# Feed-forward layers with seven products for eight: the third weight sum moved from VectorE to an accumulating DMA, and a new table of spacings

## Chip, cores and metric

One core of a Trainium2 chip. The time is device microseconds (us) for one execution of the whole kernel, as the median of several runs; lower is better. The engines are named as the profile names them: PE (TensorE, matmuls), ACT (ScalarE), DVE (VectorE), POOL (GpSimd) and SP (the engine that issues most DMAs).

## What is computed

Two decoder layers over 256 tokens of width 2048 in float32: attention with its projections, and behind each attention a feed-forward part. The change is in that last part alone:

```python
D_MODEL = 2048
SEQ = 256
D_FF = -(-(8 * D_MODEL) // (3 * 256)) * 256        # 5632

def swiglu(h, w_gate, w_up, w_down):
    return (jax.nn.silu(h @ w_gate) * (h @ w_up)) @ w_down

# in layer_a and in layer_b alike, behind the attention:
    h = h + o
    return h + swiglu(rms_norm(h, norm_ffn), w_gate, w_up, w_down)
```

The tokens' activations stay on the chip; every weight is read once from memory and used for all 256 tokens.

## The kernel before

**Three matmuls for one product.** To keep float32 accuracy each operand is split into a high and a low part. `split` does it with two instructions: ACT rounds (`hi`), and DVE subtracts (`lo`, line 81). `mm3` then runs hi x hi, lo x hi and hi x lo (lines 89 to 91). PE has 512 columns in each of these matmuls. A split of a 128x1024 weight tile gives `whi` and `wlo`, one of a whole quarter gives `qhi` and `qlo` (128x2048 where four pairs of rows are taken together, 128x1536 where it is three).

**Groups.** The 5632 columns of the hidden layer are eleven blocks of 512, in three portions of four, four and three blocks (`PORTIONS`). A gate/up group computes one block: four PSUM banks (two halves of the tokens, gate and up). After the blocks of a portion, two down groups multiply that portion's hidden values with `w_down` and add to `h`. So the row of groups in a layer is: gate/up 0 to 3, down, down, gate/up 4 to 7, down, down, gate/up 8 to 10, down, down. In layer b the last portion's down projection is made by plain matmuls at the very end (`final`).

**Seven products for eight.** In a group some pairs of 128-row blocks (`npr` pairs: 4 in a gate/up group, `NPH` = 3 in a down group) are not multiplied as four times two blocks but by a scheme of seven products on sums of blocks. The remaining rows are "chunks": each chunk is one 128x1024 weight tile and 12 matmuls (`plain`). A gate/up group has 8 chunks (the first of a layer 16, and no products), a down group has 10 (6 in the last portion). The seven products are the steps `s0` to `s6`. Each needs a weight operand made from the four quarters q11, q12, q22 and q21 in tiles `qa`, `qb` and `qc`, which are loaded by SP (1024 KB for a gate/up group, 768 KB for a down group):

- `s0`: q11 in `qa`
- `s1`: `qa` + q12 (a DVE addition)
- `s2`: `qa` + q22 (a DVE addition); then POOL issues a DMA that adds q21 from memory onto `qa`
- `s3`: q12 + q22 in `qb` (a DVE addition)
- `s4`: q22 in `qc`;  `s5`: `qa` with q21 added;  `s6`: q21, loaded into `qb`

There is one buffer of each of `qa`, `qb` and `qc`, two of `qhi`/`qlo`, three of `whi`/`wlo` and four of the raw chunks. So the q11 of the next group is loaded into `qa` only when DVE has made the `qlo` of `s5`, and a split waits until PE has finished the product, or the chunk three back, whose buffer it takes.

**What sets the order.** `run_groups` runs the chunks of group g interleaved with the seven steps of group g+1: the table in `spacing` says how many chunks stand ahead of `s0`, `s1`, ... `s6`. With 8 chunks it was (2, 1, 1, 2, 0, 2, 0), so the order on PE was two chunks, `s0`, one chunk, `s1`, one chunk, `s2`, two chunks, `s3`, `s4`, two chunks, `s5`, `s6`, and then the next group's first chunks. PE's order is that of the code; the other engines' and SP's order comes from a scheduler at build time, and each engine runs its list strictly in order. `done` finishes a group: for a gate/up group two silu and two multiplications, after which `heads` transposes the new hidden values during the next group (from its sixth tick on; a tick is a third of a chunk's 12 matmuls or one row pair of a product) and, for a pair of rows that takes part in the seven products, forms their sums on DVE (lines 287 to 290, `xf`). For a down group `done` is four additions onto `h` (line 1036, or line 335 in the last portion). `keep`, `rest` and the copies from bank to bank combine the products.

Of the kernel before, what the change touches and what calls it, by code (L numbers as in the profile page):

```python
# [44 lines left out]
def decoder_trunk(ctx: ExitStack, tc: tile.TileContext, a: dict, out: bass.AP):  # L45
# [126 lines left out]
    def at(fs, *ticks):  # L172
        assert len(fs) == len(ticks)
        return list(zip(ticks, fs))
# [678 lines left out]
    class Group:  # L853
# [4 lines left out]

        late = False

        def __init__(self, op, quarters, rest, done, rest_done=None):
            self.op, self.q, self.rest, self.done, self.rest_done = op, quarters, rest, done, rest_done
            self.bank = {}
            self.r = None
            self.plain_only = quarters is None
            if quarters is None:
                for i in range(3):
                    self.new(i)
# [11 lines left out]
        def product(self, b, s, t, side, start=False):  # L880
# [3 lines left out]
            for q in range(npr):  # L884
                mm3(self.bank[b], self.op.slot(q, s), tuple(v[:, q * 512:(q + 1) * 512] for v in hl),
                    start and q == 0, q == npr - 1, True)
                side.tick()

        def keep(self, b):
            t = fq.tile([P, 512], F32, tag="keep", name="keep", bufs=2)  # L890
            with tc.high_priority(offset=URGENT):
                nc.scalar.activation(t, self.bank[b], AF.Copy)
            return t

        def steps(self, side):
            def s0():
                self.qa = self.load(0)
                self.new(1)
                self.product(1, 1, self.qa, side, True)
                with tc.high_priority(offset=URGENT):  # L900
                    nc.scalar.activation(self.new(0), self.bank[1], AF.Copy)

            def s1():
                self.qb = self.load(1)
                nc.vector.tensor_add(self.qa, self.qa, self.qb)
                self.new(2)
                self.product(2, 7, self.qa, side, True)
                self.p5 = self.keep(2)

# [9 lines left out]
            def s3():  # L919
                nc.vector.tensor_add(self.qb, self.qb, self.qc)  # L920
                self.product(1, 4, self.qb, side)
                self.r = fq.tile([P, 512], F32, tag="rest", name="rest")
                with tc.high_priority(offset=URGENT):
                    nc.vector.tensor_sub(self.r, self.p5, self.bank[1])
                if self.rest_done is not None:
                    self.rest_done(self)
# [30 lines left out]

    def spacing(n, late):

        if late:  # L960
            return (4, 1, 0, 1, 0, 2, 0), n - 8
        base = {16: (4, 2, 2, 3, 2, 3, 0), 10: (3, 1, 1, 2, 1, 2, 0), 8: (2, 1, 1, 2, 0, 2, 0), 6: (1, 1, 0, 1, 1, 2, 0)}[n]
        return base, n - sum(base)

    def run_groups(groups):
        for i, g in enumerate(groups):
# [4 lines left out]
            if nxt is not None and nxt.q is not None:  # L971
                base, left = spacing(n, nxt.late)
                for p, s in enumerate(nxt.steps(side)):
                    for _ in range(base[p] + (left if p == 6 else 0)):
                        g.plain(c, side)
                        c += 1
                    if c == n and g.done is not None:
                        side.flush()
                        g.done(g)
                        g.done = None  # L980
                    s()
# [7 lines left out]
    def ffn(pre, op, f_r, last):  # L989
        gq, gs = a[pre + "_gu_q"], a[pre + "_gu_s"]  # L990
        groups = []
        for pi, (b0, b1) in enumerate(PORTIONS):
# [4 lines left out]
            def hop(pi=pi, nk=nk, final=final, hp=hp):  # L997
                if "op" not in hp:
                    x = pair(lambda i: fh.tile([P, HW], F32R, tag=("hThi", "hTlo")[i], name=("hThi", "hTlo")[i]))
                    hp["op"] = Paired(x, NPH, nk, sums=not (final and pre == "b"))  # L1000
                return hp["op"]

            def gate_up(g, j, hop=hop, late=b1 - b0 < 4):
                hb = []
                for tt in range(2):
# [3 lines left out]
                    hb.append(t)  # L1009
                deferred.extend(at(hop().heads(j, hb), *((4, 4) if late and j > 0 else (6, 6))))  # L1010

# [6 lines left out]
            if final and pre == "b":  # L1018
                run_groups(groups)
                last([[a["b_w_down_last"][nb, c] for c in range(nk // CK)] for nb in range(4)], hop().xs, nk)  # L1020
                return
            dq, ds = a[f"{pre}_dn_q"], a[f"{pre}_dn_s{pi}"]
            for n2 in range(2):
# [13 lines left out]

                groups.append(Lazy(n2 == 0 and b1 - b0 < 4, hop, [dq[pi, n2, i] for i in range(4)], [ds[n2, c] for c in range(nk - 2 * NPH)], done, rest_done))
        run_groups(groups)

    class Lazy(Group):
        def __init__(self, late, hop, *args):
            super().__init__(None, *args)
            self.late, self.hop = late, hop

# [228 lines left out]
def _layout(np, i):  # L1274
# [24 lines left out]
    for pre in "ab":  # L1299
# [3 lines left out]
        g[pre + "_gu_q"], g[pre + "_gu_s"] = q[1:], r[1:]  # L1303
        dq = []
        for pi, (b0, b1) in enumerate(PORTIONS):
            w = wd[b0 * 512:b1 * 512].reshape(-1, 2, 2, 512)
            q, r, _ = _pairs(np, w[:, :, 0].reshape(-1, 1024), w[:, :, 1].reshape(-1, 1024), 2, NPH)
            if pre == "b" and pi == len(PORTIONS) - 1:
                g["b_w_down_last"] = _blocks(np, wd[b0 * 512:b1 * 512])
            else:  # L1310
                dq.append(q)
                g[f"{pre}_dn_s{pi}"] = r
        g[pre + "_dn_q"] = np.stack(dq)
    return g
# [26 lines left out]
```

## Time and profile before

| | |
|---|---|
| median of 3 runs | 2041.65 us (2041.49 to 2043.13) |
| the profiled execution | 2039.75 us; its span, first to last instruction, 2038.0 us |
| PE busy | 2006.9 us, 98% of the span |
| DVE busy | 1620.9 us, 80% |
| ACT busy | 1216.3 us, 60% |
| DMA queues | 55.1% (SP's) and 8.3% (POOL's) of the 16 DMA engines' span |

A busy share is an average over stages. "PE busy" counts an engine that has a matmul in flight, and matmuls overlap, so what a wait costs is read from the distance between two matmuls' starts.

### The profile page before, as it was taken

The numbers are of one execution on the slowest core, as the hardware profiler recorded it, in microseconds if no ns is written. First come the engines' busy times: TensorE is split into PE (matmuls) and PEld (weight loads), VectorE is DVE, ScalarE is ACT, GpSimd is POOL, SyncE is SP. The second block draws the span as 40 slices with busy tenths as digits, with TensorE's granted clock in tenths as the row PEclk, the third lists the DMA queues.
The fourth block names the chain that finished last, engine by engine and source line by source line (L and its number), as shares of the span: only waits on it lengthen the run. The fifth ranks groups of instructions, "written<-read, shape, count | busy, mean of one in ns | idle before, by whom it ended". The sixth has DMA issues, their size and how long they took to land.

```text
span 2038.0 us, 25320 instructions
## 1 busy us (share of the span) xinstructions
PE 2006.9 (98%) x9357; PEld 1664.7 (82%) x9357; DVE 1620.9 (80%) x1975; ACT 1216.3 (60%) x1534; POOL 37.2 (2%) x62
## 2 busy tenths in 40 slices
PE   9999999999999999999999999999999999999998
PEld 7898888888888888888887888878888888888886
DVE  6767898778888888888887678788888888888855
ACT  7755566656655566555665555666655566655643
POOL 0000000000000000000000000000000000000000
PEclk9999999999999999999999999999999999999999
DMA  8867633576666676567764754476656776567654
GB/s 309 275 197 232 215 124 116 185 245 213 245 203 218 217 243 238 192 217 225 252 215 136 238 166 156 147 254 217 235 190 211 233 255 224 189 214 242 211 188 150
DMA packets 103100, 429.56 MB, mean 211 GB/s; under 512 B 11968, under 2 KB 12352, under 8 KB 89792
## 3 DMA queue, kind: packets, MB, share of 16 engines
q1 hardware_dynamic: 97632, 395.31, 55.1%
q0 software_dynamic: 5056, 31.59, 8.3%
q8 instruction: 73, 1.20, 0.2%
q10 hardware_dynamic: 288, 1.05, 0.1%
q14 instruction: 51, 0.42, 0.1%
HBM read 423.71 MB, written 4.19 MB: 210 GB/s over the span
## 4 chain that ended last, share of the span: by engine, by line
PE 86%; DVE 8%; issue 2%; ACT 2%; DMA 1%; SPq 0%; POOLq 0%; POOL 0%; ACTq 0%; DVEq 0%
PE mm L91 27%; PE mm L89 27%; PE mm L90 27%; DVE qlo L81 3%; DVE wlo L81 1%; DVE q L920 1%; PE aux L235 1%; ACT qhi L80 1%; DMA q<-in_a_dn_q_dram 1%; PE aux L91 1%; DVE hTlo L81 1%; PE aux L90 1%; PE aux L89 1%; PE aux L316 1%; PE aux L350 0%
## 5 line engine op out<-in xcount | busy, mean ns | idle before, releaser
L80 ACT ACTIVATE whi<-raw 128x1024 fp32r<-128x1024 f32 (+1 forms) x436 | 455.5, 1045 | 408.5 <-PE mm L90 343.6
L81 DVE TENSOR_TENSOR wlo<-raw,whi 128x1024 fp32r<-128x1024 f32 (+1 forms) x436 | 523.7, 1204 | 155.7 <-ACT whi L80 148.7
L81 DVE TENSOR_TENSOR qlo<-q,qhi 128x2048 fp32r<-128x2048 f32 (+1 forms) x210 | 443.1, 2112 | 138.5 <-ACT qhi L80 138.4
L80 ACT ACTIVATE qhi<-q 128x2048 fp32r<-128x2048 f32 (+1 forms) x210 | 372.2, 1775 | 196.3 <-PE mm L90 139.0
L89 PE MATMUL mm<-whi,xhi 128*128 128x512 f32 (+1 forms) x1216 | 474.2, 390 | 3.7 <-ACT xf L304 1.7
L91 PE MATMUL mm<-wlo,xhi 128*128 128x512 f32 (+1 forms) x1216 | 468.4, 385 | 0.0
L90 PE MATMUL mm<-whi,xlo 128*128 128x512 f32 (+1 forms) x1216 | 468.0, 385 | 0.0
L89 PEld LDWEIGHTS mm<-whi,xhi 128*128 128x128 f32 x1216 | 228.7, 188 | 46.2 <-ACT xf L304 2.1
L91 PEld LDWEIGHTS mm<-wlo,xhi 128*128 128x128 f32 x1216 | 228.5, 188 | 46.0
L90 PEld LDWEIGHTS mm<-whi,xlo 128*128 128x128 f32 x1216 | 228.9, 188 | 41.3
L91 PE MATMUL mm<-qlo,xhi 128*128 128x512 f32 x560 | 219.8, 393 | 9.1 <-DVE qlo L81 9.1
L89 PE MATMUL mm<-qhi,xhi 128*128 128x512 f32 x560 | 218.4, 390 | 0.0
L90 PE MATMUL mm<-qhi,xlo 128*128 128x512 f32 x560 | 218.2, 390 | 0.0
L89 PE MATMUL mm<-whi,hThi 128*128 128x512 f32 x464 | 181.5, 391 | 0.0
L91 PE MATMUL mm<-wlo,hThi 128*128 128x512 f32 x464 | 180.9, 390 | 0.0
L90 PE MATMUL mm<-whi,hTlo 128*128 128x512 f32 x464 | 180.8, 390 | 0.0
L84 DVE SCALAR_TENSOR_TENSOR wlo<-raw,gains,whi 128x512 fp32r<-128x512 f32 x160 | 113.8, 748 | 42.9 <-ACT whi L83 42.0
L83 ACT ACTIVATE whi<-raw,gains 128x512 fp32r<-128x512 f32 x160 | 107.6, 716 | 55.9 <-PE mm L90 45.1
L91 PEld LDWEIGHTS mm<-qlo,xhi 128*128 128x128 f32 x560 | 105.2, 188 | 36.4 <-DVE qlo L81 15.0
L90 PEld LDWEIGHTS mm<-qhi,xlo 128*128 128x128 f32 x560 | 105.2, 188 | 22.0
L89 PEld LDWEIGHTS mm<-qhi,xhi 128*128 128x128 f32 x560 | 105.2, 188 | 21.7 <-ACT qhi L80 0.4
L89 PE MATMUL mm<-whi,ohi 128*128 128x512 f32 x256 | 101.6, 397 | 1.6 <-ACT whi L83 1.6
(277 smaller groups left out, 2473.8 us busy)
## 6 DMA issues: line engine op xcount, KB each, us to landing
q<-in_a_gu_q_dram SPq DMA_DIRECT2D x40, 1024.0 KB, 7.0
raw<-in_a_gu_s_dram SPq DMA_DIRECT2D x80, 512.0 KB, 5.0
q<-in_b_gu_q_dram SPq DMA_DIRECT2D x40, 1024.0 KB, 7.0
raw<-in_b_gu_s_dram SPq DMA_DIRECT2D x80, 512.0 KB, 5.2
raw<-in_a_dn_s_dram SPq DMA_DIRECT2D x52, 512.0 KB, 4.6
raw<-in_b_dn_s_dram SPq DMA_DIRECT2D x40, 512.0 KB, 4.8
q<-in_a_dn_q_dram SPq DMA_DIRECT2D x24, 768.0 KB, 5.9
raw<-in_a_w_out_dram SPq DMA_DIRECT2D x32, 512.0 KB, 3.7
```

The lines of the kernel that those rows point to most:

```text
L80: nc.scalar.activation(hi, src, AF.Copy)
L81: nc.vector.tensor_sub(lo, src, hi.bitcast(F32))
L83: nc.scalar.activation(hi, src, AF.Copy, scale=gain)
L84: nc.vector.scalar_tensor_tensor(lo, src, gain, hi.bitcast(F32), op0=ALU.mult, op1=ALU.subtract)
L89: nc.tensor.matmul(o, l[0], r[0], start=start, stop=False, skip_group_check=more)
L90: nc.tensor.matmul(o, l[1], r[0], start=False, stop=False, skip_group_check=more)
L91: nc.tensor.matmul(o, l[0], r[1], start=False, stop=stop, skip_group_check=more)
L235: nc.tensor.transpose(ps[:, i * P:(i + 1) * P], s, ident)
L316: nc.tensor.transpose(ps[:, i * P:(i + 1) * P], tok[tt][:, i * P:(i + 1) * P], ident)
L920: nc.vector.tensor_add(self.qb, self.qb, self.qc)
```

## The change

The sum q12 + q22 is no longer made by DVE: right behind the addition that uses q12, POOL issues a second DMA that adds the third quarter from memory onto `qb`. The table of spacings is new, with no separate one for the last portion. The last portion's down groups take two row pairs into the seven products in place of three (`NPH - final`), so they have 8 chunks, a quarter there has 512 KB, and the weights are laid out accordingly. The load of the first q11 of a layer stands ahead of that layer's first chunks in the code (`fetch`).

```diff
+        def fetch(self):
+            self.qa = self.load(0)
+
...
             def s0():
-                self.qa = self.load(0)
+                if self.qa is None:
+                    self.fetch()
                 self.new(1)
                 self.product(1, 1, self.qa, side, True)
...
                 nc.vector.tensor_add(self.qa, self.qa, self.qb)
                 self.new(2)
                 self.product(2, 7, self.qa, side, True)
+                nc.gpsimd.dma_start(self.qb, self.q[2], accum_op=ALU.add)
                 self.p5 = self.keep(2)
...
             def s3():
-                nc.vector.tensor_add(self.qb, self.qb, self.qc)
                 self.product(1, 4, self.qb, side)
...
-    def spacing(n, late):
-
-        if late:
-            return (4, 1, 0, 1, 0, 2, 0), n - 8
-        base = {16: (4, 2, 2, 3, 2, 3, 0), 10: (3, 1, 1, 2, 1, 2, 0), 8: (2, 1, 1, 2, 0, 2, 0), 6: (1, 1, 0, 1, 1, 2, 0)}[n]
-        return base, n - sum(base)
+    def spacing(n):
+
+
+        return {16: (4, 3, 3, 3, 1, 2, 0), 10: (2, 2, 2, 2, 1, 1, 0), 8: (1, 2, 2, 2, 0, 1, 0)}[n]
...
             if nxt is not None and nxt.q is not None:
-                base, left = spacing(n, nxt.late)
-                for p, s in enumerate(nxt.steps(side)):
-                    for _ in range(base[p] + (left if p == 6 else 0)):
+                if g.plain_only:
+                    nxt.fetch()
+                for ahead, s in zip(spacing(n), nxt.steps(side)):
+                    for _ in range(ahead):
...
-                    hp["op"] = Paired(x, NPH, nk, sums=not (final and pre == "b"))
+                    hp["op"] = Paired(x, NPH - final, nk, sums=not (final and pre == "b"))
...
-                deferred.extend(at(hop().heads(j, hb), *((4, 4) if late and j > 0 else (6, 6))))
+                deferred.extend(at(hop().heads(j, hb), 6, 6))
```

**First place: DVE, from `s0` to `s2`.** Layer a, while the third gate/up group's chunks run and the next group's products are made. `qlo_5292` (before) and `qlo_5249` (after) belong to `s0`, `qlo_5332` to `s1`, and `qlo_5371` (before) and `qlo_5390` (after) to `s2`; `hTlo` and `xf` are the hidden values of the block before. Before:

```order
L81 TENSOR_TENSOR qlo_5292<-q11_5288,qhi_5291 128x2048
L905 TENSOR_TENSOR q11_5288<-q11_5288,q12_5327 128x2048
L81 TENSOR_TENSOR wlo_5352<-raw_5349,whi_5351 128x1024
L920 TENSOR_TENSOR q12_5327<-q12_5327,q22_5367 128x2048
L81 TENSOR_TENSOR hTlo_4882<-aux_5257,hThi_4881 128x2x128
L81 TENSOR_TENSOR hTlo_4882<-xf_5262,hThi_4881 128x512
L81 TENSOR_TENSOR hTlo_4882<-aux_5266,hThi_4881 128x2x128
L287 TENSOR_TENSOR xf_5262<-xf_5262 128x128
L81 TENSOR_TENSOR qlo_5332<-q11_5288,qhi_5331 128x2048
L288 TENSOR_TENSOR xf_5262<-xf_5262 128x128
L912 TENSOR_TENSOR q11_5288<-q11_5288,q22_5367 128x2048
```

After, from the same step on:

```order
L81 TENSOR_TENSOR qlo_5249<-q11_5245,qhi_5248 128x2048
L907 TENSOR_TENSOR q11_5245<-q11_5245,q12_5327 128x2048
L81 TENSOR_TENSOR wlo_5353<-raw_5350,whi_5352 128x1024
L81 TENSOR_TENSOR hTlo_4882<-aux_5258,hThi_4881 128x2x128
L81 TENSOR_TENSOR hTlo_4882<-aux_5267,hThi_4881 128x2x128
L81 TENSOR_TENSOR hTlo_4882<-xf_5263,hThi_4881 128x512
L287 TENSOR_TENSOR xf_5263<-xf_5263 128x128
L288 TENSOR_TENSOR xf_5263<-xf_5263 128x128
L289 TENSOR_TENSOR xf_5263<-xf_5263 128x128
L290 TENSOR_TENSOR xf_5263<-xf_5263 128x128
L81 TENSOR_TENSOR qlo_5332<-q11_5245,qhi_5331 128x2048
L81 TENSOR_TENSOR hTlo_4882<-xf_5263,hThi_4881 128x512
```

The addition of line 920 is gone, the hidden values' sums stand ahead of the `qlo` of `s1`, and the addition for `s2` (line 912 before, 915 after) has moved behind them.

**Second place: POOL's list of DMAs in the feed-forward part of layer a.** Before, one a group:

```order
L914 DMA q11_4558<-in_a_gu_q_dram 128x2048
L914 DMA q11_4976<-in_a_gu_q_dram 128x2048
L914 DMA q11_5288<-in_a_gu_q_dram 128x2048
L914 DMA q11_5589<-in_a_dn_q_dram 128x1536
L914 DMA q11_5887<-in_a_dn_q_dram 128x1536
```

After, two a group:

```order
L910 DMA q12_4633<-in_a_gu_q_dram 128x2048
L917 DMA q11_4467<-in_a_gu_q_dram 128x2048
L910 DMA q12_5015<-in_a_gu_q_dram 128x2048
L917 DMA q11_4937<-in_a_gu_q_dram 128x2048
L910 DMA q12_5327<-in_a_gu_q_dram 128x2048
L917 DMA q11_5245<-in_a_gu_q_dram 128x2048
```

A DMA onto `qb` (q12) now stands ahead of every one onto `qa` (q11).

**Third place: DVE at the end of the first down group of layer a's last portion.** `qlo_9392` and `qlo_9405` (before), `qlo_9381` and `qlo_9391` (after) belong to `s5` and `s6` of the second one; line 335 is the four additions onto `h` that end the first one. Before:

```order
L81 TENSOR_TENSOR qlo_9392<-q11_9198,qhi_9391 128x1536
L81 TENSOR_TENSOR wlo_9421<-raw_9418,whi_9420 128x1024
L81 TENSOR_TENSOR qlo_9405<-q21_9389,qhi_9404 128x1536
L335 TENSOR_TENSOR h_80<-mm_9165,h_80 128x512
L81 TENSOR_TENSOR wlo_9446<-raw_9443,whi_9445 128x1024
L335 TENSOR_TENSOR h_80<-mm_8988,h_80 128x512
```

After:

```order
L81 TENSOR_TENSOR qlo_9381<-q11_9152,qhi_9380 128x1024
L1028 TENSOR_TENSOR h_80<-h_80,rest_9333 128x512
L335 TENSOR_TENSOR h_80<-mm_8920,h_80 128x512
L335 TENSOR_TENSOR h_80<-mm_8895,h_80 128x512
L335 TENSOR_TENSOR h_80<-mm_8961,h_80 128x512
L335 TENSOR_TENSOR h_80<-mm_9133,h_80 128x512
L81 TENSOR_TENSOR qlo_9391<-q21_9378,qhi_9390 128x1024
```

The `qlo` of `s6` has moved from ahead of the four additions to behind them.

## Rows read from the trace of the kernel before

**Rows 1.** The page, head and first part: the span, and the busy time of each engine.

```profile
span 2038.0 us, 25320 instructions
PE 2006.9 (98%) x9357; PEld 1664.7 (82%) x9357; DVE 1620.9 (80%) x1975; ACT 1216.3 (60%) x1534; POOL 37.2 (2%) x62
```

**Rows 2.** Who PE waited for (us in all, times, longest): first the entry for the splits' `lo` part over the whole span, then of 420 to 1030 us, of 1030 to 1100 us (two entries), of 1330 to 1345 us and of 1345 us to the end.

```profile
PE mm L91 <- DVE qlo L81: 10.7, 16, 1.6
...
PE mm L91 <- DVE qlo L81: 4.0, 7, 1.0
...
PE mm L91 <- DVE qlo L81: 1.6, 2, 1.1
PE mm L89 <- ACT qhi L80: 1.5, 1, 1.5
...
PE mm L91 <- DVE qlo L81: 1.6, 1, 1.6
...
PE mm L91 <- DVE qlo L81: 3.5, 6, 1.0
```

**Rows 3.** Timeline of PE (start, duration, instruction; in brackets the idle time before it and what ended it): the first and the last of 36 matmuls in a stretch without a wait, and the matmuls around one wait.

```profile
469.54 0.39 PE L89 MATMUL mm<-whi,xhi 128*128 128x512 f32 x1
...
477.48 0.39 PE L91 MATMUL mm<-qlo,xhi 128*128 128x512 f32 x1
...
540.44 0.39 PE L90 MATMUL mm<-qhi,xlo 128*128 128x512 f32 x1
541.82 0.50 PE L91 MATMUL mm<-qlo,xhi 128*128 128x512 f32 x1 [0.99 <-DVE qlo L81]
542.16 0.39 PE L89 MATMUL mm<-qhi,xhi 128*128 128x512 f32 x1
```

**Rows 4.** The chain of work that ended last, 525 to 543 us (start, duration, what).

```profile
527.93 2.29 DVE q L920
...
531.69 2.20 DVE qlo L81
...
539.57 2.21 DVE qlo L81
```

**Rows 5.** Groups of instructions by line and shape (count | busy us, mean ns of one | idle before).

```profile
L81 DVE TENSOR_TENSOR wlo<-raw,whi 128x1024 fp32r<-128x1024 f32 x420 | 512.0, 1222 | 144.1 <-ACT whi L80 137.1 <-PE mm L91 3.3 <-PE aux L301 2.2
...
L920 DVE TENSOR_TENSOR q<-q,q 128x2048 f32<-128x2048 f32 x20 | 45.7, 2286 | 0.0
...
L335 DVE TENSOR_TENSOR h<-mm,h 128x512 f32<-128x512 f32 x24 | 15.9, 685 | 0.7 <-PE mm L91 0.5
...
L920 DVE TENSOR_TENSOR q<-q,q 128x1536 f32<-128x1536 f32 x10 | 17.6, 1758 | 0.3
```

**Rows 6.** Busy time of each engine, first from one wait to the next, a whole group, then in its part from the end of DVE's `qlo` of `s0` to the end of that of `s2` (stretch and its length, busy us and instructions of each engine, granted clock, DMA share, GB/s).

```profile
498.83:541.82 42.99, 42.00 (x188) 34.56 (x188) 38.48 (x33) 27.89 (x28) 0.89 (x1) 1.00 0.66 224
...
524.55:541.78 17.23, 16.28 (x76) 13.23 (x75) 17.20 (x17) 12.64 (x15) 0.00 (x0) 1.00 0.26 79
```

**Rows 7.** Timelines of ACT and of DVE: the split of `s5` in the group that ends at 518 us.

```profile
509.38 1.92 ACT L80 ACTIVATE qhi<-q 128x2048 fp32r<-128x2048 f32 x1 [1.66 <-PE mm L90]
...
511.33 2.29 DVE L81 TENSOR_TENSOR qlo<-q,qhi 128x2048 fp32r<-128x2048 f32 x1 [1.04 <-ACT qhi L80]
```

**Rows 8.** From issue to landing, in us: first the median of all 40 loads of gate/up quarters in a layer, then single loads of line 877: that of q11 into `qa` in eight groups (issued at 513.65, 723.54, 765.99, 975.94, 1426.33, 1636.24, 1678.69 and 1888.63 us, in order 5.1, 4.8, 6.3, 5.5, 5.3, 6.1, 4.8 and 6.4; the second 4.8, 5.5 and 5.3 have no row of their own), and last that of q21 issued at 501.34 us.

```profile
q<-in_a_gu_q_dram SPq DMA_DIRECT2D x40, 1024.0 KB, 7.0
...
DMA to landing us min/median/max: 5.1/5.1/5.1
...
DMA to landing us min/median/max: 4.8/4.8/4.8
...
DMA to landing us min/median/max: 6.3/6.3/6.3
...
DMA to landing us min/median/max: 6.1/6.1/6.1
...
DMA to landing us min/median/max: 6.4/6.4/6.4
...
DMA to landing us min/median/max: 8.6/8.6/8.6
```

**Rows 9.** The accumulating DMAs of line 914: one issue on POOL (timeline), its time from issue to landing, and that of all thirty (min, median, max).

```profile
499.08 0.89 POOL L914 DMA_DIRECT2D q<-in_a_gu_q_dram  x1 [52.77 <-DVE qlo L81]
...
DMA to landing us min/median/max: 9.6/9.6/9.6
...
DMA to landing us min/median/max: 7.7/9.1/11.6
```

**Rows 10.** The chain of work that ended last, 1065 to 1081 us: layer a's last portion, while the first down group's six chunks run.

```profile
1066.62 1.77 DVE q L905
...
1068.41 1.76 DVE q L920
...
1074.20 1.77 DVE q L912
```

**Rows 11.** The start of layer b's feed-forward part: timelines of DVE and of SP.

```profile
1331.14 0.69 DVE L81 TENSOR_TENSOR xlo<-xf,xhi 128x512 fp32r<-128x512 f32 x1
...
1331.91 0.80 SPq L877 DMA_DIRECT2D q<-in_b_gu_q_dram  x2
...
1339.36 2.29 DVE L81 TENSOR_TENSOR qlo<-q,qhi 128x2048 fp32r<-128x2048 f32 x1 [0.58 <-ACT qhi L80]
```

More of the change, by code (lines that the diff above doesn't have):

```diff
@@ L853, in decoder_trunk @@
     class Group:
-        late = False
         def __init__(self, op, quarters, rest, done, rest_done=None):
@@ L863, in __init__ @@
             self.bank = {}
-            self.r = None
+            self.r = self.qa = None
             self.plain_only = quarters is None
@@ L999, in hop, with gate_up @@
                     x = pair(lambda i: fh.tile([P, HW], F32R, tag=("hThi", "hTlo")[i], name=("hThi", "hTlo")[i]))
-                    hp["op"] = Paired(x, NPH, nk, sums=not (final and pre == "b"))
+                    hp["op"] = Paired(x, NPH - final, nk, sums=not (final and pre == "b"))
                 return hp["op"]
-            def gate_up(g, j, hop=hop, late=b1 - b0 < 4):
+            def gate_up(g, j, hop=hop):
                 hb = []
@@ L1021, in ffn @@
                 return
-            dq, ds = a[f"{pre}_dn_q"], a[f"{pre}_dn_s{pi}"]
+            npr = NPH - final
+            dq, ds = a[f"{pre}_dn_q{pi}"], a[f"{pre}_dn_s{pi}"]
             for n2 in range(2):
@@ L1036, in done, with __init__ @@
                                 nc.vector.tensor_add(hbk, ps[tt], hbk)
-                groups.append(Lazy(n2 == 0 and b1 - b0 < 4, hop, [dq[pi, n2, i] for i in range(4)], [ds[n2, c] for c in range(nk - 2 * NPH)], done, rest_done))
+                groups.append(Lazy(hop, [dq[n2, i] for i in range(4)], [ds[n2, c] for c in range(nk - 2 * npr)], done, rest_done))
         run_groups(groups)
     class Lazy(Group):
-        def __init__(self, late, hop, *args):
+        def __init__(self, hop, *args):
             super().__init__(None, *args)
-            self.late, self.hop = late, hop
+            self.hop = hop
         def steps(self, side):
@@ L1303, in _layout @@
         g[pre + "_gu_q"], g[pre + "_gu_s"] = q[1:], r[1:]
-        dq = []
         for pi, (b0, b1) in enumerate(PORTIONS):
+            final = pi == len(PORTIONS) - 1
             w = wd[b0 * 512:b1 * 512].reshape(-1, 2, 2, 512)
-            q, r, _ = _pairs(np, w[:, :, 0].reshape(-1, 1024), w[:, :, 1].reshape(-1, 1024), 2, NPH)
-            if pre == "b" and pi == len(PORTIONS) - 1:
+            q, r, _ = _pairs(np, w[:, :, 0].reshape(-1, 1024), w[:, :, 1].reshape(-1, 1024), 2, NPH - final)
+            if pre == "b" and final:
                 g["b_w_down_last"] = _blocks(np, wd[b0 * 512:b1 * 512])
             else:
-                dq.append(q)
-                g[f"{pre}_dn_s{pi}"] = r
-        g[pre + "_dn_q"] = np.stack(dq)
+                g[f"{pre}_dn_q{pi}"], g[f"{pre}_dn_s{pi}"] = q, r
     return g
```

## The prediction

> **What bounds the kernel now.** The page's head comes first: PE has a matmul in flight in 98% of the span, DVE works in 80% [rows 1]. So the time is PE's list of matmuls, plus the places where PE stands still, and the change can gain only what is lost in the latter. Second, the list of whom PE waited for: the entry for the `lo` part of a split is 10.7 us in 16 waits, with one wait of 1.5 us for a `hi` part beside it [rows 2]. By stretch they are 4.0 us in 7 waits in layer a's gate/up groups, 3.5 in 6 in layer b's, 1.6 in 2 and the 1.5 in layer a's last portion, and one of 1.6 at the start of layer b's feed-forward part [rows 2]. Third, the timeline, for what a wait costs: without waits PE starts a matmul every (477.48 - 469.54) / 35 = 0.227 us, while two steps around a wait took 1.72 us for a shown gap of 0.99 [rows 3]; 1.72 - 0.45 = 1.27, so a wait costs its gap and 0.28 more. That makes 12.2 + 17 x 0.28 = 17.0 us lost in the groups that are changed.
>
> Fourth, what ended last ahead of a wait. The chain into the wait at 541.82 is DVE alone: the addition of line 920 at 527.93, the `qlo` of `s1`, the addition of line 912, and the `qlo` of `s2` from 539.57 [rows 4]. From the end of `s0`'s `qlo` to the end of `s2`'s, DVE was busy for 17.20 of 17.23 us [rows 6], while PE's order has four units of 12 matmuls there (`s0`, a chunk, `s1`, a chunk), 48 x 0.227 = 10.9 us and the transposes. Over a whole group DVE has only 38.48 of 42.99 us [rows 6]: it is not the bound on average, it is late in that one stretch. In layer a's last portion lines 905, 920 and 912 stand in the chain in the same way [rows 10].
>
> **The addition that is removed.** Line 920 takes 2.29 us in 20 groups and 1.76 in ten [rows 5], 63 us of DVE. By itself that is worth nothing; what counts is the stretch. After the change DVE's list there has lost line 920 (2.29) and one `wlo` (1.22 [rows 5]), and the addition for `s2` stands directly ahead of the split of `s2`, so ACT's `qhi` (1.92 [rows 7]) is now on the path: 17.23 - 2.29 - 1.22 + 1.92 = 15.6 us. PE has two chunks more in the same stretch: 72 x 0.227 = 16.3, and 0.45 to the third matmul, the first that needs `qlo`. The data comes about 1.1 us early; the transposes add to that. The 13 waits of the gate/up groups should go: 7.5 + 13 x 0.28 = **11.1 us gained**.
>
> In the last portion both changes work together. A split or a sum there is 128x1024, 1.22 us by the `wlo` of that shape [rows 5]; two `qlo`, two sums, two `wlo` and a `qhi` of a like time are about 8.5 us against 8 chunks' spacing, (24 + 24 + 12) x 0.227 = 13.6. Its three waits go: 3.1 + 3 x 0.28 = **3.9 us gained**. Fewer row pairs cost matmuls: 8 x 12 + 7 x 6 = 138 in place of 6 x 12 + 7 x 9 = 135, in two groups 6 x 0.227 = **1.4 us lost**.
>
> The wait at the start of layer b stays. It follows from the load of q11 at 1331.91, right behind DVE's `xlo` that ended at 1331.83, and the `qlo` at 1339.36 [rows 11]. The load stands at the same place of SP's list after the change, so `fetch` is costed at nothing, with no other work needed to hide it.
>
> **The DMA that is added.** It is issued at the end of the addition ahead of it. The thirty like it took 7.7 to 11.6 us, median 9.1, and 0.89 of POOL, which does little else [rows 1, 9]. Its result is wanted by the `qhi` of `s3`, ahead of which nothing waits on ACT and DVE but behind which stand the two chunks between `s2` and `s3`. PE reaches these 84 matmuls after `s0`'s `qlo`, 19.0 us; the addition takes 2.29 of it; `qhi`, `qlo` and `wlo` need 1.92 + 2.29 + 1.22 = 5.4; with 0.45 to the third matmul, a landing within 11.8 us costs nothing. I take zero; even the longest seen has 0.2 to spare, but the median is what I go by. If this cover fails, PE waits for a `wlo`, at the excess plus 0.28, in up to 30 groups. The other accumulation, q21 onto `qa`, landed 0.70 us before the split that uses it (499.08 + 9.6, then 509.38 [rows 7, 9]); it has as many matmuls of time as before, and the data of `s2` now comes about 1.1 us before PE wants it, so the spare time grows.
>
> **Where the stall goes.** The new table has one chunk ahead of `s0` and one ahead of `s5`, so it takes PE's time from the border between two groups and gives it to the middle. There the q11 of the next group can be loaded only after the `qlo` of `s5`. That split starts when PE has finished `s3`, whose buffer it takes, and ends 4.27 us later (509.38 to 513.62 [rows 7]). Then comes the load, L, and then `s0`'s split, 1.92 + 2.29 and about 0.15 of hand-offs. PE's order from the end of `s3` to `s0` is now `s4`, a chunk, `s5`, `s6`, a chunk: 60 x 0.227 = 13.6, and 0.45 more, 14.05 (it was 84 matmuls). So L may be at most 14.05 - 4.27 - 4.36 = 5.4 us. Eight borders lie between two gate/up groups and have this length; the rest have a quarter of 768 KB or less, or more matmuls. At these eight, L was 5.1, 4.8, 6.3, 5.5, 5.3, 6.1, 4.8 and 6.4 [rows 8]. Unchanged it would cost 0.9 + 0.1 + 0.7 + 1.0 and four times 0.28, 3.8 us. In its favour the accumulation ahead of it now runs earlier relative to the border; against it one more raw chunk is queued there. Bounds are 0 (every load within 5.4) and 15.0 (all at 7.0, the median of the quarters [rows 8]). The eight rows are this very load, so I stay near them and take **2.2 us lost**.
>
> **A new place.** At the end of the first down group of layer a's last portion the `qlo` of `s6` now stands behind the four additions of line 335. The last of these needs the last chunk's last matmul: 0.39 in flight [rows 3], some 0.3 of hand-off, 0.685 [rows 5], then the `qlo` of 1.22: 2.6 to 2.7 us after the chunk. PE wants it after `s5`'s 6 matmuls, 1.36 + 0.45 = 1.81. That is 0.9 + 0.28 = **1.2 us lost**, once. Its bounds are 0 and the four additions in full, 2.7.
>
> **The sum.** -11.1 - 3.9 + 1.4 + 2.2 + 1.2 = -10.2 us on the profiled execution of 2039.75 (span 2038.0 and 1.75 around it): 2029.5. The median of the three runs lies 1.9 higher, which I add: 2031.5.
>
> **Rival A: the border eats the gain.** Every load at 7.0 costs 8 x (1.6 + 0.28) = 15.0 in place of 2.2: 2044.3. The gain falls under 0.2% (4.1 us, about what a measurement of this kernel can tell from no change) from L = 6.2 and is gone at 6.7. For it: the median of all quarters. Against it: none of the eight exceeded 6.4.
>
> **Rival B: slower.** The accumulations took 8.3% of the DMA engines' time by the table of the page; another thirty add nearly as much, where the DMA share in a group is 0.66 already [rows 6]. If q11 then lands as late as the q21 issued at 501.34 behind an accumulation, 8.6 us [rows 8], the border costs 8 x (3.2 + 0.28) = 27.8 in place of 2.2: 2057. It makes the kernel slower by 0.2% from L = 7.2. Against it: the new DMA is issued some 20 us ahead of the border and has landed when q11 is asked for.
>
> **Rival C: POOL's DMA comes late.** In this kernel an accumulation was issued at 499.08 while DVE ran a `qlo`, and landed after 9.6, near the median [rows 9]. If one behind other DVE work waited for two of its instructions, 9.1 + 2 x 2.29 = 13.7, the excess of 1.9 + 0.28 in the 20 gate/up groups would cost 44 us: 2075. It decides from 11.8 us on. The Trainium skill ("SBUF — State Buffer", section "SBUF: two separate sides") warns of this: descriptors of a DMA issued from GpSimd cannot be written while VectorE runs a two-port operation. Its section "Who interferes with whom" says that a tensor_tensor has no such mode, and DVE's list here consists of these; by that the trace agrees, with its 9.6 beside a median of 9.1.
>
> **Rival D: nothing is relieved.** If the waits come from the order of hand-offs between PE, ACT and DVE and not from DVE's work, they stay, and 1.4 + 1.2 are added: 2044. Against it: DVE had no idle time in the stretch [rows 6].
>
> **How the numbers follow.** The forecast has a chance of 0.68, A 0.14, D 0.09, B 0.06, C 0.03. The forecast's own range is 2027 (no new wait at the border or the new place: -13.6, and a little for the median) to 2036 (the border at 3.8, the new place at 2.7, and a third of the middle's waits left at half their size). With the part of A up to L = 6.8 and half of D it is 2027 to 2043, which leaves out under 2 in 10. Faster: the forecast and a third of A, 0.72; same: the rest of A and most of D, 0.16; slower: B, C and what A and D hold above 2045.7, 0.12.
>
> **What would show it.** PE's waits for `qlo` and `qhi` fall from 12.2 us in 17 to about 4; none is left with line 915 ahead of it; the wait of 1.6 at the start of layer b is still there; one of about 0.9 with line 335 ahead of it is new. The period of a gate/up group falls from 42.99 to about 41.8 us. The DMAs of line 910 land within 11.8 us, and ACT never waits for them. The eight loads of q11 show L near 5.4. The prediction is wrong if L passes 6.2, if ACT waits for POOL's DMA, or if DVE's stretch from `s0` to `s2` takes over 16.8 us.

## The result, and the profile after

The changed kernel takes 2030.95 us, median of 4 runs (2029.22 to 2033.42), beside 2041.57 for the kernel before: a ratio of 0.9948, 95% interval 0.9931 to 0.9965. The profiled execution took 2029.28 us. Measured once more, beside others (below), it took 2030.31 us, ratio 0.9950 (0.9937 to 0.9962). The forecast was 2031.5 us, 2029.5 for a profiled execution.

The page after, head, first part and DMA queues, against [rows 1]:

```profile
span 2027.5 us, 25444 instructions
...
PE 2004.9 (99%) x9363; PEld 1665.5 (82%) x9363; DVE 1556.5 (77%) x1942; ACT 1208.1 (60%) x1531; POOL 63.6 (3%) x92
...
q1 hardware_dynamic: 98208, 395.31, 56.2%
q0 software_dynamic: 9376, 59.38, 15.4%
```

DVE lost 64 us of work, POOL's DMAs went from 8.3% to 15.4% of the DMA engines' time, and PE has six matmuls more. Where the span's 10.5 us went is seen in whom PE waited for, against [rows 2]: first the whole span, then 420 to 1030 us, 1030 to 1100, 1320 to 1345, and 1345 to the end.

```profile
PE mm L91 <- DVE qlo L81: 3.7, 4, 1.6
...
PE mm L91 <- DVE qlo L81: 0.6, 1, 0.6
...
PE mm L91 <- DVE qlo L81: 0.8, 1, 0.8
...
PE mm L91 <- DVE qlo L81: 1.6, 1, 1.6
...
PE mm L91 <- DVE qlo L81: 0.8, 1, 0.8
```

Of 17 waits (12.2 us) four are left (3.7 us), and each has a place that was named ahead: two at a border between two gate/up groups (0.6 and 0.8), one behind line 335 (0.8), one at the start of layer b (1.6). With 0.28 for each, 17.0 us became 4.8: 12.2 less, and 1.4 more for the matmuls makes 10.8 against 10.5 measured.

The border, by the loads of q11 in the eight groups (issue to landing), those that landed last; then PE at the first of the two waits and POOL's new DMA:

```profile
DMA to landing us min/median/max: 6.1/6.1/6.1
...
DMA to landing us min/median/max: 6.4/6.4/6.4
...
775.77 0.50 PE L91 MATMUL mm<-qlo,xhi 128*128 128x512 f32 x1 [0.56 <-DVE qlo L81]
...
DMA to landing us min/median/max: 5.2/9.8/11.2
...
  ACT qhi L80: 8.1, 8
```

The loads issued at 765.23 and 1671.17 us took 6.1 and 6.4 us; the other six took 4.7 to 5.3. Against the limit of 5.4 that makes 0.7 and 1.0; 0.6 and 0.8 were measured, at just these two (0.4 and 0.9 when the same kernel was profiled again). The last two rows are of line 910: its DMAs landed within 11.2 us, and eight of them were waited for by ACT's `qhi`, for 8.1 us in all, while PE in these groups waited four times only, as above.

The new place is seen in DVE's and PE's timelines (start, duration, instruction), the end of the first down group of layer a's last portion:

```profile
1083.25 2.48 DVE L335 TENSOR_TENSOR h<-mm,h 128x512 f32<-128x512 f32 x4
1085.64 1.21 DVE L81 TENSOR_TENSOR qlo<-q,qhi 128x1024 fp32r<-128x1024 f32 x1
...
1086.91 0.50 PE L91 MATMUL mm<-qlo,hThi 128*128 128x512 f32 x1 [0.79 <-DVE qlo L81]
```

The four additions end at 1085.7, `qlo` directly behind them at 1086.85, and PE stood 0.79 us.

### The profile page after: what moved, and what is told of

It reads as the page before. It is cut to its first block, busy times and chain, and to the rows that moved or that the text cites. A ratio compares the mean times of both kernels' runs of the same rounds, so it can differ in the third digit from the quotient of the medians.

```text
span 2027.5 us, 25444 instructions
## 1 busy us (share of the span) xinstructions
PE 2004.9 (99%) x9363; PEld 1665.5 (82%) x9363; DVE 1556.5 (77%) x1942; ACT 1208.1 (60%) x1531; POOL 63.6 (3%) x92
## 3 DMA queue, kind: packets, MB, share of 16 engines
q1 hardware_dynamic: 98208, 395.31, 56.2%
q0 software_dynamic: 9376, 59.38, 15.4%
## 4 chain that ended last, share of the span: by engine, by line
PE 94%; DVE 2%; DMA 1%; ACT 1%; issue 0%; SPq 0%; POOLq 0%; POOL 0%; ACTq 0%; DVEq 0%
PE mm L91 30%; PE mm L89 30%; PE mm L90 29%; PE aux L316 1%; PE aux L235 1%; PE aux L91 1%; PE aux L90 1%; DVE qlo L81 1%; PE aux L89 1%; DMA q<-in_b_gu_q_dram 1%; DVE wlo L81 0%; ACT qhi L80 0%; PE aux L350 0%; PE cmp L639 0%; PE cmp L638 0%
## 5 line engine op out<-in xcount | busy, mean ns | idle before, releaser
L81 DVE TENSOR_TENSOR qlo<-q,qhi 128x2048 fp32r<-128x2048 f32 (+2 forms) x210 | 436.1, 2077 | 165.4 <-ACT qhi L80 160.3
L80 ACT ACTIVATE qhi<-q 128x2048 fp32r<-128x2048 f32 (+2 forms) x210 | 366.8, 1747 | 239.8 <-PE mm L90 117.4
L89 PE MATMUL mm<-whi,hThi 128*128 128x512 f32 x480 | 187.6, 391 | 0.0
L91 PE MATMUL mm<-wlo,hThi 128*128 128x512 f32 x480 | 186.9, 389 | 0.0
L90 PE MATMUL mm<-whi,hTlo 128*128 128x512 f32 x480 | 186.8, 389 | 0.0
L91 PEld LDWEIGHTS mm<-wlo,hThi 128*128 128x128 f32 x480 | 90.1, 188 | 18.7
```

The costliest lines, as they stand in the source:

```text
L80: nc.scalar.activation(hi, src, AF.Copy)
L81: nc.vector.tensor_sub(lo, src, hi.bitcast(F32))
L89: nc.tensor.matmul(o, l[0], r[0], start=start, stop=False, skip_group_check=more)
L90: nc.tensor.matmul(o, l[1], r[0], start=False, stop=False, skip_group_check=more)
L91: nc.tensor.matmul(o, l[0], r[1], start=False, stop=stop, skip_group_check=more)
```

## Experiments

The result alone does not say which edit did it. The prediction credits the stretch between `s0` and `s2` with both the removed addition and the two more chunks of PE's work. The first five runs take the change apart.

**Third sum by DMA, spacings of before.**

```diff
-        return {16: (4, 3, 3, 3, 1, 2, 0), 10: (2, 2, 2, 2, 1, 1, 0), 8: (1, 2, 2, 2, 0, 1, 0)}[n]
+        return {16: (4, 2, 2, 3, 2, 3, 0), 10: (3, 1, 1, 2, 1, 2, 0), 8: (2, 1, 1, 2, 0, 2, 0)}[n]
```

> The changed kernel with the spacings of before (8 chunks: 2,1,1,2,0,2,0; 10: 3,1,1,2,1,2,0; 16: 4,2,2,3,2,3,0); only the third sum by DMA and the 512 KB quarters stay. Theory 1 (one ledger over the whole group): the longer border gives s0's split 84 matmuls, so it comes L-dependent 10.8 - 5.5 = 5.3 us ahead of need, and the middle may use this up; before, DVE took 17.2 us against 12.2 of PE there, 5.0 of the 5.3, which is why waits were short and only in some groups; without line 920 it is 14.9, 2.7 of 5.3. So no wait in any group, the two border waits of the changed kernel (0.6 and 0.8) gone too: profiled time about 2.0 us under that of the changed kernel, 2027.3. Theory 2 (the stretch by itself, as the prediction priced it): 14.9 us of DVE against 10.9 + 0.45 + transposes leaves a wait of about 2.7 us in each of 13 or more groups, +35 us or more: 2064 or above. Rival 3: POOL's DMA is wanted earlier in this order and lands too late: ACT's qhi and then PE wait, some 0.8 + 0.28 us in up to 30 groups, up to +32 us.

Measured: 2026.7 us (2026.06 to 2027.6), ratio 0.9927 (0.9912 to 0.9942), profiled 2027.25. That is theory 1 to a tenth. Whom PE waited for, longest first, over the whole span:

```profile
PE mm L89 <- ACT xf L304: 1.7, 1, 1.7
PE mm L91 <- DVE qlo L81: 1.6, 1, 1.6
```

The first is of the attention part, as before; the second is layer b's start. Nothing else in the feed-forward groups waits. ACT's `qhi` did wait for POOL's DMA nine times (8.4 us in all), but PE not once, so rival 3 is out. To see why, follow one group: the third gate/up group of layer a. The lead of a split is the time from the end of its `qlo` to the start of the matmul that reads it. For each kernel the rows show DVE's `qlo` of `s0`, PE's first matmul that reads it, `qlo` of `s2` and PE's first matmul of that. Before, the first pair; the second is in [rows 3] and [rows 4], 541.82 and its wait:

```profile
522.26 2.29 DVE L81 TENSOR_TENSOR qlo<-q,qhi 128x2048 fp32r<-128x2048 f32 x1 [1.90 <-ACT qhi L80]
...
529.79 0.39 PE L91 MATMUL mm<-qlo,xhi 128*128 128x512 f32 x1
```

The kernel old_order, and the stretch between the ends of the two `qlo` (length, then busy us and instructions of PE, PEld, DVE, ACT, POOL, granted clock, DMA share, GB/s):

```profile
521.10 2.29 DVE L81 TENSOR_TENSOR qlo<-q,qhi 128x2048 fp32r<-128x2048 f32 x1 [1.91 <-ACT qhi L80]
...
528.63 0.39 PE L91 MATMUL mm<-qlo,xhi 128*128 128x512 f32 x1
...
535.72 2.29 DVE L81 TENSOR_TENSOR qlo<-q,qhi 128x2048 fp32r<-128x2048 f32 x1
...
539.51 0.39 PE L91 MATMUL mm<-qlo,xhi 128*128 128x512 f32 x1
...
523.39:538.01 14.62, 14.62 (x70) 12.18 (x70) 13.52 (x15) 10.36 (x14) 0.88 (x1) 1.00 0.65 143
```

The changed kernel:

```profile
522.23 2.29 DVE L81 TENSOR_TENSOR qlo<-q,qhi 128x2048 fp32r<-128x2048 f32 x1 [1.57 <-ACT qhi L80]
...
525.31 0.39 PE L91 MATMUL mm<-qlo,xhi 128*128 128x512 f32 x1
...
538.74 2.29 DVE L81 TENSOR_TENSOR qlo<-q,qhi 128x2048 fp32r<-128x2048 f32 x1 [0.85 <-ACT qhi L80]
...
542.53 0.39 PE L91 MATMUL mm<-qlo,xhi 128*128 128x512 f32 x1
...
524.52:541.03 16.51, 16.51 (x79) 13.76 (x78) 15.49 (x17) 11.88 (x15) 0.88 (x1) 1.00 0.65 160
```

Before, `s0`'s `qlo` ended at 524.55 and was read at 529.79, a lead of 5.2 us. The stretch then took 17.2 us where PE, from the one reader to the other, has 10.9 (48 matmuls; in old_order, where nothing waits, 528.63 to 539.51): 6.3 more, which is the lead and 1.1 besides, a wait of 1.0 at `s2`. The expectation's 12.2 for PE was too much. With the addition gone the stretch is 14.6, 3.7 more than PE's, and 1.5 us of the lead are left at `s2` (538.01, read at 539.51). In the changed kernel the lead at `s0` is only 0.8 (524.52 to 525.31), because two chunks less stand ahead of it in PE's order, and it grows to 1.5 by `s2` (541.03 to 542.53), because two more stand behind it. So border and middle are one account: a chunk taken from the border to the middle gives the middle what it takes from the border, and with the addition gone the middle did not need it.

**Third sum on DVE again, new spacings.**

```diff
             def s1():
...
-                nc.gpsimd.dma_start(self.qb, self.q[2], accum_op=ALU.add)
...
             def s3():
+                nc.vector.tensor_add(self.qb, self.qb, self.qc)
                 self.product(1, 4, self.qb, side)
```

> The changed kernel with the third sum back on DVE and no second accumulating DMA; the new spacings and the 512 KB quarters stay. Theory 1 (ledger over the whole group): the border leaves s0's split 5.4 us minus L, about nothing, and the middle takes 15.6 + 2.3 = 17.9 us of DVE against 17.6 of PE, so waits of 0.3 to 1.5 us and 0.28 each in the eight gate/up groups behind another, about 8 us of them, and less elsewhere: 2036 to 2041 by the profile, most of the gain lost. Theory 2 (the spacing alone is what relieves, DVE's work is not): waits as in the changed kernel, 2029 to 2031.

Measured: 2032.41 us (2030.95 to 2034.54), ratio 0.9952 (0.9935 to 0.9969). PE's waits over the span:

```profile
PE mm L91 <- DVE qlo L81: 5.1, 5, 1.6
```

The same group, `s0` and `s2`, each with the `qlo` and its reader:

```profile
525.40 2.29 DVE L81 TENSOR_TENSOR qlo<-q,qhi 128x2048 fp32r<-128x2048 f32 x1 [2.26 <-ACT qhi L80]
...
527.81 0.44 PE L91 MATMUL mm<-qlo,xhi 128*128 128x512 f32 x1
...
542.76 2.29 DVE L81 TENSOR_TENSOR qlo<-q,qhi 128x2048 fp32r<-128x2048 f32 x1 [0.65 <-ACT qhi L80]
...
545.42 0.39 PE L91 MATMUL mm<-qlo,xhi 128*128 128x512 f32 x1
```

Neither theory's number: five waits of 5.1 us where the changed kernel has four of 3.7, 1.7 us more, not the 5 to 11 that theory 1 forecast. The account holds in kind: the lead is 0.1 at `s0` (the `qlo` ends at 527.69, PE reads it at 527.81) and 0.4 at `s2`, so the middle gains 0.3, where I had it lose 0.3, and makes no waits of its own. All of the 1.7 us is at the border: three waits of 2.7 us, behind loads of q11 of 6.1 to 6.8 us, in place of two of 1.4. These loads differ between executions of one kernel too, so it is not shown that the sum on DVE costs anything here. The new spacings alone are thus nearly enough too.

**Both undone**, with only the last portion's two row pairs left of the change.

```diff
-        return {16: (4, 3, 3, 3, 1, 2, 0), 10: (2, 2, 2, 2, 1, 1, 0), 8: (1, 2, 2, 2, 0, 1, 0)}[n]
+        return {16: (4, 2, 2, 3, 2, 3, 0), 10: (3, 1, 1, 2, 1, 2, 0), 8: (2, 1, 1, 2, 0, 2, 0)}[n]
...
-                nc.gpsimd.dma_start(self.qb, self.q[2], accum_op=ALU.add)
...
+                nc.vector.tensor_add(self.qb, self.qb, self.qc)
```

> The changed kernel with the spacings of before and the third sum on DVE: what stays of the change is the last portion of layer a (two row pairs, 8 chunks) and the load of q11 in the code. Ledger: s0's split has its lead of 5.2 us and DVE uses up 5.1 of it by s2, so the 13 waits of the gate/up groups stay (7.5 + 3.6 us); the 6 more matmuls cost 1.4; the three waits of the last portion go at most (3.9). So 2036.5 to 2040 by the profile, which shows both other parts without effect outside the last portion.

Measured: 2037.76 us (2036.74 to 2039.49), ratio 0.9983 (0.9973 to 0.9992). PE's waits, the whole span, then 420 to 1030 us and 1345 us to the end:

```profile
PE mm L91 <- DVE qlo L81: 9.1, 14, 1.6
...
PE mm L91 <- DVE qlo L81: 4.0, 7, 1.0
...
PE mm L91 <- DVE qlo L81: 3.5, 6, 1.0
```

The 13 waits are those of [rows 2] to the tenth; only the last portion's are gone. With this the four corners are known, all with two row pairs: 2037.8 with neither edit, 2026.7 with the DMA alone, 2032.4 with the spacings alone, 2030.3 to 2031.0 with both. The two edits relieve the same stretch and do not add; with the DMA in place the new spacings cost about 4 us by the medians, 2.9 by the waits (three of 2.1 us in all, and 0.28 each).

**The last portion with three row pairs**, first with the spacing for 6 chunks alone, then exactly as before.

```diff
-        return {16: (4, 3, 3, 3, 1, 2, 0), 10: (2, 2, 2, 2, 1, 1, 0), 8: (1, 2, 2, 2, 0, 1, 0)}[n]
+        return {16: (4, 3, 3, 3, 1, 2, 0), 10: (2, 2, 2, 2, 1, 1, 0), 8: (1, 2, 2, 2, 0, 1, 0), 6: (1, 1, 0, 1, 1, 2, 0)}[n]
...
-                    hp["op"] = Paired(x, NPH - final, nk, sums=not (final and pre == "b"))
+                    hp["op"] = Paired(x, NPH, nk, sums=not (final and pre == "b"))
...
-            npr = NPH - final
+            npr = NPH
```

> The changed kernel with three row pairs again in the last portion's down groups of layer a (6 chunks, 768 KB quarters; spacing for 6 chunks 1,1,0,1,1,2,0 as before, without the separate table for that portion). Theory: 6 matmuls fewer, -1.4 us; without line 920 the chain that made the waits of 1.6 + 1.5 us is 1.8 us shorter, but s1 and s2 follow one another without a chunk, so POOL's DMA is wanted some 8.8 us after it starts and PE waits where it lands later: waits of 0 to 3 us in that group, and the wait of 0.8 behind line 335 stays or falls away with the order. Net between -2.5 and +2.5 us against the changed kernel. Rival: the removed sum alone is enough there, no wait left, -1.4 us or better, and the smaller row pairs only cost.

Measured: 2038.79 us (2036.91 to 2041.01), ratio 0.9986 (0.9977 to 0.9995). That is 7.8 us over the changed kernel, outside the range, and not for the reasons given. PE's waits from 1030 to 1100 us:

```profile
PE mm L89 <- ACT hThi L80: 2.7, 1, 2.7
PE mm L90 <- DVE hTlo L81: 1.2, 1, 1.2
PE mm L91 <- DVE qlo L81: 1.1, 1, 1.1
PE mm L89 <- ACT qhi L80: 0.9, 1, 0.9
PE mm L89 <- DVE hTlo L81: 0.9, 1, 0.9
```

The hidden values `hThi` and `hTlo` come late: the smaller groups were paired, before, with transposes from the fourth tick on and a spacing of their own, and this run had neither. The second run restores both:

```diff
-    def spacing(n):
+    def spacing(n, late):
...
+        if late:
+            return (4, 1, 0, 1, 0, 2, 0)
...
-                deferred.extend(at(hop().heads(j, hb), 6, 6))
+                deferred.extend(at(hop().heads(j, hb), *((4, 4) if late and j > 0 else (6, 6))))
```

> The changed kernel with the last portion of layer a exactly as before (three row pairs, 6 chunks, its own spacing 4,1,0,1,0,2,0 ahead of it, hidden values transposed from the fourth tick on). Ledger: 1.4 us of matmuls less and the 1.1 of line 335 gone; but between s0 and the split of s3 PE has only 39 to 48 matmuls (8.8 to 10.9 us), and a DMA of 768 KB that lands after 6.6 to 9.4 us behind an addition of 1.77 us is 0 to 5 us late for the chunk behind s2. So waits of 1 to 6 us in that group by qhi or qlo of s3 and what is queued behind it, and a total within -1.5 to +3.5 us of the changed kernel. The 6.8 us of waits that the run npr3 had there on the transposed hidden values (hThi, hTlo) should be gone, as they were of the sixth tick. Rival: those waits stay.

Measured: 2030.78 us (2030.31 to 2033.19), beside 2030.31 for the changed kernel in the same comparison. PE's waits in the same window:

```profile
PE mm L91 <- DVE qlo L81: 1.1, 1, 1.1
PE mm L91 <- DVE wlo L81: 1.0, 1, 1.0
PE mm L89 <- ACT qhi L80: 0.7, 1, 0.7
```

In place of the changed kernel's one wait of 0.8 there, three of 2.8 us in all stand: 2.0 + 2 x 0.28 = 2.6 more against 1.4 of matmuls less, so 1.2 us by the waits, too little for the medians to tell. Those for `qhi` and `qlo` (1.8 us) are of `s2` and follow DVE's addition ahead of it; the expectation had put them behind POOL's DMA. The DMA alone does not clear this place: before, the three waits were 3.1 us [rows 2], and with the DMA and three row pairs they are 2.8. Here the fewer row pairs did it, with the table for 8 chunks and the smaller quarters that come with them; these were not tried apart.

**One chunk from the middle back to the border.**

```diff
-        return {16: (4, 3, 3, 3, 1, 2, 0), 10: (2, 2, 2, 2, 1, 1, 0), 8: (1, 2, 2, 2, 0, 1, 0)}[n]
+        return {16: (4, 3, 3, 3, 1, 2, 0), 10: (2, 2, 2, 2, 1, 1, 0), 8: (2, 2, 2, 1, 0, 1, 0)}[n]
```

> The changed kernel with one chunk moved from between s2 and s3 to ahead of s0 where there are 8 chunks (2,2,2,1,0,1,0). Ledger: the border has 72 matmuls in place of 60, so L may be up to 8.1 us if the split of s5 starts as early as now; but s3 ends 12 matmuls earlier after s2, and the accumulation of q21 (8.7 to 10.6 us) may then be what s5's split waits for, which takes back up to 1.5 us: limit 6.6 or more, over the longest L of 6.4. So the two border waits (0.6 and 0.8) go: about -2.0 us against the changed kernel. Rival: the accumulations' landing now sets s5's split in most groups and PE waits for the qlo of s5 or of s0, +0.5 to +1 us in each of 8 groups, +4 to +8.

Measured: 2029.8 us (2027.36 to 2030.54), profiled 2027.36, 1.9 under the changed kernel's profile. The waits at the border are gone; those of line 335 (0.8) and of layer b's start (1.6) are left. The medians alone don't tell it from the changed kernel; the waits do.

**The additions of line 335 behind the split of `s6`.**

```diff
-                    if c == n and g.done is not None:
+                    if c == n and g.done is not None and not (n == 8 and isinstance(g, Lazy)):
```

> The changed kernel with the four additions of line 335 at the end of layer a's last portion put behind the split of s6 in the code, so that on DVE the qlo of s6 stands ahead of them again; nothing else moves. Theory: the wait of 0.8 us between 1030 and 1100 us goes, and with it 0.8 + 0.28 = 1.1 us; the other three waits stay. Rival: the wait is not of the additions but of the last chunk's end, and stays.

Measured by one profiled execution, 2027.79 us, so the trace has to tell: no wait is left between 1030 and 1100 us, and the other three places still wait (0.9, 1.6 and 0.2). On DVE the `qlo` of `s6` now starts at 1083.55 and the four additions stand behind it, at 1084.68. The wait was that of the additions.

**One chunk more ahead of `s0` at a layer's start, on top of old_order** (the lines against old_order).

```diff
-        return {16: (4, 2, 2, 3, 2, 3, 0), 10: (3, 1, 1, 2, 1, 2, 0), 8: (2, 1, 1, 2, 0, 2, 0)}[n]
+        return {16: (5, 2, 2, 3, 2, 2, 0), 10: (3, 1, 1, 2, 1, 2, 0), 8: (2, 1, 1, 2, 0, 2, 0)}[n]
```

> The kernel old_order (third sum by DMA, spacings of before) with one chunk more ahead of s0 at the start of a layer: 16 chunks as 5,2,2,3,2,2,0. The only wait left in old_order's feed-forward groups is the 1.6 us at the start of layer b, behind the load of q11. One chunk is 12 x 0.227 = 2.7 us of matmuls ahead of s0, so it goes: 1.6 + 0.28 = 1.9 us less, profiled time about 2025.4. Rival: the chunk is moved from ahead of s5, and the next border or the first split's chunks are then late, no gain or 1 to 2 us back.

> The changed kernel unaltered, on the same chip as the three beside it. By the waits of the profiles it should take about 2.9 us more than old_order and 4.8 more than old_order_start: 2029 to 2031.

Measured together: 2024.27 us (2023.89 to 2025.21), ratio 0.9917 (0.9904 to 0.9931), and 2030.31 (2028.94 to 2034.31) for the changed kernel. The wait of 1.6 is gone and no feed-forward group waits for a split; the profiled time was 2025.21, against 2025.4 forecast. This version beats both kernels: 17 us under the one before, 6 under the changed one.

**How late POOL's DMA may land.** Small additions on POOL ahead of each DMA of line 910 (four, then twelve):

```diff
+                dl = fq.tile([P, 128], F32, tag="dly", name="dly", bufs=1)
+                for d in range(4):
+                    nc.gpsimd.tensor_add(dl, self.qa[:, :128], self.qb[:, :128])
                 nc.gpsimd.dma_start(self.qb, self.q[2], accum_op=ALU.add)
```

> The changed kernel with four small additions on POOL (128x128, first columns of qa and qb into a spare tile) ahead of each new accumulating DMA, so that it is issued some 2 us later behind the addition of line 907. The prediction's limit: a landing 11.8 us after that addition, plus the lead that s0's split has (0.1 to 1.6 us in the eight groups behind another gate/up group, more elsewhere), costs nothing. 9.8 + 2 is at the limit: 0 to +6 us against the changed kernel, ACT's waits for the DMA grow by some 1 to 2 us in each group. Rival (the limit is the lead that s3's own qlo shows, 4.9 us and more): no wait of PE added. Both fail if POOL's additions slow DVE's instructions beside them.

> The same with twelve small additions, some 6 us of delay, landing at about 15.8 us. The prediction's limit: 15.8 - 11.8 - 1 = 3 us and 0.28 in each of the eight tight groups, 0 to 2.5 in the other twenty or so: +30 to +60 us against the changed kernel, with PE waiting for wlo of the first chunk behind s2, which ACT and DVE make behind the split of s3. Rival (limit is the lead of s3's own qlo, 4.9 to 15 us in the changed kernel): waits of about 1 us for that qlo in the three groups with 4.9, +4 us at most.

Measured: 2042.18 us (2039.5 to 2046.54) and 2150.36 us (2142.0 to 2156.09), some 11 and 120 us over the changed kernel and both beyond what was expected. The delay was longer than meant. With four additions, POOL in one group, then the landing of all thirty, then PE's waits for a `lo` part, and last the split of `s3` in the group shown, the `wlo` behind it and PE:

```profile
952.96 5.11 POOL L912 TENSOR_TENSOR dly<-q,q 128x128 f32<-128x128 f32 x4 [33.10 <-DVE q L907]
958.48 0.89 POOL L913 DMA_DIRECT2D q<-in_a_gu_q_dram  x1 [0.41 <-POOL dly L912]
...
DMA to landing us min/median/max: 5.2/8.2/10.7
...
PE mm L91 <- DVE qlo L81: 7.7, 7, 1.6
PE mm L91 <- DVE wlo L81: 4.1, 5, 1.3
...
968.40 1.92 ACT L80 ACTIVATE qhi<-q 128x2048 fp32r<-128x2048 f32 x1 [5.05 <-DMA q<-in_a_gu_q_dram]
...
972.56 2.35 DVE L81 TENSOR_TENSOR wlo<-raw,whi 128x1024 fp32r<-128x1024 f32 x2
...
973.84 0.50 PE L91 MATMUL mm<-wlo,xhi 128*128 128x512 f32 x1 [1.30 <-DVE wlo L81]
```

The DMA leaves 5.6 us behind the end of its addition here (952.88 to 958.48); in the changed kernel it leaves 0.64 behind it, by the median. Counted from the end of the addition, the thirty land after 13.1 us (median; 17.1 at the longest), in the changed kernel after 10.5 (11.8). PE now waits five times for a `wlo`, 4.1 us in all. In each of the five, ACT's `qhi` of `s3` had waited 3.6 to 5.9 us for the DMA, and the `whi` and `wlo` behind it came late: that is the order of the prediction, and the rival (only `s3`'s own `qlo` counts) has no place for it.

These five waits are only half of the 11 us. Five more, 5.3 us in all where the changed kernel has two of 1.4, are at the border, behind loads of q11 that took 6.1 to 7.1 us; why these took longer is not shown. So landings of up to 11.8 us were free and some later ones cost PE time, but how exact the limit is stays open: the five groups that wait had landings after 14.0 to 17.1 us, others of up to 17.0 had no wait, and the additions also held up DVE's sum for `s2` (7.9 us in all waiting for POOL), whose columns they read. With twelve that confound is too large (114.4 us) to read a limit from the 120 us.

## Why the prediction was right, point by point

- **The middle, 11.1 gained.** The 13 waits went, and the period of a gate/up group fell to 41.7 us, forecast at 41.8. The data of `s2`, forecast some 1.1 us early (16.3 + 0.45 - 15.6), was 1.5 early in the group above (17.2 + 0.8 - 16.5), by errors that cancel. The stretch took 16.5 us, not 15.6: three `wlo` stand in it before and after, so none fell out, and DVE stood idle 1.0 us for `qhi`, not 1.92. PE took 17.2, not 16.3: the transposes had no price. That the difference came out is luck in part. And the working named only half of the account: it set 17.2 us of DVE against 10.9 of PE, which would have meant waits of some 6 us before the change, where [rows 2] has at most 1.0. The lead of 5.2 us at `s0` was missing. With it, the text would have seen that 14.9 us without line 920 already fit into 10.9 + 5.2, and that the new table gives up a lead that was not in the way.
- **The border, 2.2 lost.** Measured 0.6 + 0.8 + 2 x 0.28 = 2.0, at the two loads above 5.4. The 2.2 was chosen between bounds, not worked out. Rivals A and B needed loads of 6.2 or 7.2 throughout; the longest was 6.4. Twice the accumulations did not slow these loads: 4.7 to 6.4 after, 4.8 to 6.4 before [rows 8]. They are not without effect: the gate/up chunks, 512 KB each, landed after 5.0 us (layer a) and 5.2 (layer b) by the median before and 6.7 after, with 6.1 and 6.2 in old_order and 6.0 and 5.7 in sum_dve, so both edits have a part. PE waited for none of these.
- **The new place, 1.2 lost.** Measured 0.79 + 0.28 = 1.1, and shown to be line 335 by moving it. The working had the last addition 0.3 behind the chunk's last matmul, for a hand-off that no run shows; it started 0.7 behind it, because the four ran back to back from 1083.25.
- **The start of layer b.** Stayed at 1.6, as said; it was removed by one chunk.
- **The added DMA, nothing lost.** Landings of 5.2 to 11.2 us against the limit of 11.8, but the text counted from the end of the addition, and the DMA left 0.64 behind that: counted so, 10.5 by the median and 11.8 at the longest, just at the limit. The lead at `s0`, also left out, adds to the limit (0.8 in the group above). Rival C did not occur: the new DMAs' median was 9.8, beside 9.1 for those of before [rows 9], with DVE at work beside them.
- **The signs.** "ACT never waits for them" was wrong: it did eight times, 8.1 us, and PE waited for none of it. By the letter two of the three signs of being wrong came, this one and a load over 6.2 us (one of eight, 6.4); both were drawn too tight. The third, a stretch over 16.8 us, did not, by 0.3.
- **The last portion.** All three waits went, for 1.4 us of matmuls: 2.5 gained by the sum, 3.4 by the medians of old_sum and of the kernel before beside it (2041.13). Set back to three row pairs, 2.8 us of waits returned. The prediction credited both edits there; the DMA had a small part.

## What to carry to other kernels

A wait names the instruction that came last, not the stretch that spent the lead: follow the lead (end of the producer to start of its reader) from step to step through a whole period, and count where it is earned and where it is used. Two edits that relieve the same stretch don't add; take the one that costs nothing elsewhere, here the addition given to the DMA engines, and leave the order as it was. An order that is moved to shield one stretch takes the shield from another.

## What the runs showed of the hardware

POOL's queue, nearly all of it accumulating DMAs, takes more of the DMA engines for a byte than SP's plain loads: 59.38 MB were 15.4% of their time and 395.31 MB 56.2%, 0.26 and 0.14% for a MB. Whether the adding or the queue costs this, the runs do not separate. And POOL's small additions, all of 128x128, took between 0.45 and 2.59 us; the 56 that took over 0.6 us all ran beside an instruction of DVE. The row of all 120 (min, median and max in ns), and a `wlo` of DVE beside one of them:

```profile
L912 POOL TENSOR_TENSOR dly<-q,q x120: 449/464/2588, 433.2 to 1907.5; 128x128 f32<-128x128 f32 x120
...
910.10 1.49 DVE L81 TENSOR_TENSOR wlo<-raw,whi 128x1024 fp32r<-128x1024 f32 x1
```

The Trainium skill ("SBUF — State Buffer", section "Who interferes with whom") says that a VectorE instruction with two inputs in SBUF contends with a GpSimd instruction that reads SBUF; the trace agrees. Mostly POOL waited, by up to 2.1 us; DVE did too, by up to 0.3: four `wlo` took 1.48 to 1.49 us, where in the changed kernel none took more than 1.23. The landings of POOL's DMAs, at a median of 9.8, did not show the delay of rival C.
